# First projections read host-transposed rows, and the row norms are multiplied in afterwards

## The chip, the core and the metric

The kernel runs on one core of a Trainium2 chip, in one launch. The metric is device time in microseconds (us). An execution's time is a little longer than the span of its instructions: the profiled execution below took 1341.73 us and its span, from the first to the last instruction, is 1339.8 us. Engines go by the names of the profile: PE multiplies matrices, and PEld is its loading of weights; DVE is VectorE, ACT ScalarE, POOL GpSimd, and SP issues most transfers. PEclk is the clock that PE was granted, as a share of its higher level (1.00 is 2.4 GHz and 0.50 is 1.2 GHz).

## The reference

One layer of a streaming encoder over 1088 rows (1024 of a prompt, 64 of a sample) with 1024 features. Only its head matters here:

```python
def rmsnorm(x, g):
    y = x * lax.rsqrt(jnp.mean(x * x, axis=-1, keepdims=True) + EPS)
    return y * g
...
h = rmsnorm(x, g_mix)
c_q, c_kv, k_r, conv_b, conv_c, conv_x, gate_a, gate_c = split_cols(h @ w_in)
...
lat_new = rmsnorm(c_kv, g_ckv)
...
u = conv_c * conv_x
cv = sum(conv_w[k] * up[:, k:k + S] for k in range(CONV_W))   # up is u behind two earlier rows
y_c = (conv_b * cv) @ w_oc
...
m = jax.nn.sigmoid(gate_a) * y_a + jax.nn.sigmoid(gate_c) * y_c
```

Attention, an output projection, a mixture of 32 experts and a last gated embedding follow; the change leaves their code alone.

## The kernel before

**Tiles.** The 1088 rows are nine tiles of 128 rows (the last has 64). PE needs h with features on the partitions, so each tile is normalised and then transposed. The result lies in two pairs of buffers: hTA holds rows 0 to 383 (tiles 0, 1, 2; call it chunk A), hTB the rest (chunk B is rows 384 to 767, chunk C the last 320). Every fp32 operand is split into a rounded high part and a remainder (names with h and l at the end; `split`, `hi`, `lo`), and every product is three matmuls (`mm3`): high by high, low by high, high by low. `hi` is an ACT cast, `lo` a DVE subtraction.

**Steps of a tile i.** `A0` loads its rows (SP). `A1` squares and sums them on ACT (junk, L215), and POOL makes 1/rms in two instructions (rs, L85 and L86). `B` multiplies rows, 1/rms and the gain g_mix into hx (two DVE instructions; the gain is spread over the partitions beforehand by two matmuls of a row of ones with the gain, L256). `Tr` transposes hx by eight PE instructions (L237) into two banks of PSUM, and `C` splits them into hTA or hTB (two ACT casts, two DVE subtractions).

**Column tiles.** The projection's columns go through in groups of 128; `g_load` loads such a group g of w_in (w_r, 512 KB), `g_split` splits it, `g_mm` multiplies it with one chunk in 24 matmuls (eight blocks of features, three each). The first three groups are conv_c, conv_x and conv_b of the first 128 conv channels: I call their products c0, x0 and b0, with the chunk behind (c0A). They are copied, multiplied and convolved by `ev_c`, `ev_x` and `ev_b`; then a list of jobs does nine more conv groups and eight rounds of both gates (chunk A only, `ev_a` and `ev_g`). After that `L_mm` and `L_stat` make the latents, and their norms.

**What sets the order.** The text gives an order in which tiles, steps and matmuls mix by hand; a scheduler turns it into one queue for each engine, which the engine works off in order, and it decides which of the eight PSUM banks a product gets. A product whose bank is still to be read waits.

Of the kernel before, what the change touches and what calls it, by code (L numbers as in the profile page):

```python
# [7 lines left out]
F32 = mybir.dt.float32  # L8
# [3 lines left out]
AF = mybir.ActivationFunctionType  # L12
OP = mybir.AluOpType
# [7 lines left out]
D = 1024  # L21
KD = 8
# [12 lines left out]
A2 = 2 * T  # L35
DEEP = 5
WARM = 10


@with_exitstack  # L40
def body(ctx, tc, a):
# [35 lines left out]
    def split(p, raw, shape, tag, bufs, eng=None):  # L77
        h = p.tile(shape, F32R, name=tag + "h", tag=tag + "h", bufs=bufs)
        l = p.tile(shape, F32R, name=tag + "l", tag=tag + "l", bufs=bufs)
        hi(h, raw)  # L80
        lo(l, raw, h[:], eng)
        return h, l

    def rstd(out, ss, scale, n):
        nc.gpsimd.tensor_scalar(out=out, in0=ss, scalar1=scale, scalar2=EPS, op0=OP.mult, op1=OP.add)  # L85
        nc.gpsimd.tensor_tensor(out=out, in0=out, in1=mhalf[:out.shape[0], :n], op=OP.pow)  # L86

    def rstd_c(out, ss, cvec, n):
# [22 lines left out]
    def bank():  # L111
        return pb.tile([128, 512], F32, name="bk", tag="bk")
# [99 lines left out]
    def A1(i):
        junk = xp.tile([128, D], F32, name="junk")[:TN[i]]
        ss = xp.tile([128, 1], F32, name="ss", bufs=3)[:TN[i]]
        nc.scalar.activation(junk, xt_[i], AF.Square, accum_out=ss)  # L215
        rs_[i] = xp.tile([128, 1], F32, name="rs", bufs=3)[:TN[i]]
        rstd(rs_[i], ss, 1.0 / D, 1)

    hb_ = {}

    def B(i):
        hx = xp.tile([128, D], F32, name="hx", bufs=2)[:TN[i]]
        for b in range(2):
            c = slice(512 * b, 512 * b + 512)
            nc.vector.scalar_tensor_tensor(out=hx[:, c], in0=xt_[i][:, c], scalar=rs_[i], in1=gbk[b][:TN[i]],
                                           op0=OP.mult, op1=OP.mult)
        xt_.pop(i)
        hx_[i] = hx

    def Tr(i):  # L230
        hb_[i] = []
        for b in range(2):
            ps = bank()
            for j in range(4):
                k = 4 * b + j
                n = TN[i]
                nc.tensor.transpose(ps[:, 128 * j:128 * j + n], hx_[i][:, 128 * k:128 * k + 128], ident[:n, :n])  # L237
            hb_[i].append(ps)
        hx_.pop(i)

    def C(i):
        c0, n = 128 * i, TN[i]
        for b in range(2):
            v = hb_[i][b].rearrange("p (j n) -> p j n", j=4)[:, :, 0:n]
            xh, xl = hT(c0, n)
            hh = xh[:, 4 * b:4 * b + 4]
            hi(hh, v)
            lo(xl[:, 4 * b:4 * b + 4], v, hh)
            if n < 128:
                nc.gpsimd.tensor_copy(hB[0][:, 4 * b:4 * b + 4, T - TB:], xl[:, 4 * b:4 * b + 4].bitcast(F32))  # L250

    A0(0), A0(1), g_load(0), A0(2)
    A1(0), A1(1)
    gbk = [bank(), bank()]
    for b in range(2):
        nc.tensor.matmul(gbk[b], one1, grow[:, 512 * b:512 * b + 512], start=True, stop=True)  # L256
    B(0), A0(3), Tr(0), A1(2)
    B(1), Tr(1), C(0), g_load(1), A0(4), A1(3)
    g_split(0)
    B(2), Tr(2), C(1), A0(5), A1(4)  # L260
    B(3), C(2), A0(6)
    nc.sync.dma_start(stc, a["stateT"])
    nc.sync.dma_start(cw, a["convw"])
    fc, pc = ev_c(0), bank()
    g_mm(pc, *CH[0], wsp[0], hT, 0, 4, KD)
# [4 lines left out]
    fx, pxx = ev_x(0), bank()  # L270
    g_mm(pxx, *CH[0], wsp[1], hT, 0, 4, KD)
    Tr(5), B(6), C(5), A1(7)
    g_mm(pxx, *CH[0], wsp[1], hT, 4, 8, KD)
    Tr(6), B(7), C(6), A1(8)
    fx(pxx, *CH[0])
    pc = bank()
    g_mm(pc, *CH[1], wsp[0], hT, 0, 4, KD)
    Tr(7), B(8), C(7)
    g_mm(pc, *CH[1], wsp[0], hT, 4, 8, KD)
    Tr(8), C(8)  # L280
    fc(pc, *CH[1])
    xs_.close()
    pxx, pc = bank(), bank()
    g_load(2)
    g_mm(pxx, *CH[1], wsp[1], hT, 0, 8, KD)
    fx(pxx, *CH[1])
    g_split(2)
    pxx = bank()
# [157 lines left out]
    def L_stat(i):  # L446
        p1, p2 = st3[i]
        ss = lp.tile([128, 3], F32, name="ss3", bufs=2)
        cq = lp.tile([128, 256], F32, name="cq", bufs=2)
        ltk = lp.tile([128, 288], F32, name="ltk", bufs=2)  # L450
        if i == 8:
            fold(p1[:, 0:256], cq)
            fold(p2[:, 0:288], ltk)
        nc.scalar.activation(cq, p1[:, 0:256], AF.Square, accum_out=ss[:, 0:1])
        nc.scalar.activation(ltk[:, 0:256], p2[:, 0:256], AF.Square, accum_out=ss[:, 1:2])
        nc.scalar.activation(ltk[:, 256:288], p2[:, 256:288], AF.Square, accum_out=ss[:, 2:3])
        rs = lp.tile([128, 3], F32, name="rs3", bufs=2)
# [1352 lines left out]
```

## Time and profile before

| | |
|---|---|
| median of 3 runs | 1338.59 us (1335.41 to 1339.55) |
| profiled execution | 1341.73 us; span 1339.8 us |
| PE busy | 1272.8 us, 95% of the span |
| PEld, DVE, ACT, POOL busy | 82%, 63%, 49%, 24% |
| granted PE clock, mean | 0.986 |

The page of the profile cuts the span in 40 slices of 33.5 us. PE is busy for 7 tenths of the first one and of the 27th, for 8 of four others, and for 9 or more of all the rest. A row of a timeline gives an instruction's start and duration, the line of the program, the tile written and the tiles read, and in brackets how long its engine had been idle and what ended that.

### The profile page before, as it was taken

How to read it: one execution, taken by the hardware profiler on the slowest of the kernel's cores; microseconds unless marked ns; L12 is line 12 of the kernel's file. 1: busy time of each engine (PE TensorE's matmuls, PEld its weight loads, DVE VectorE, ACT ScalarE, POOL GpSimd, SP SyncE). 2: the span in 40 equal slices, each digit the busy share in tenths (PEclk: the TensorE clock that was granted, in tenths of full speed). 3: DMA queues.
4: the chain of work that ended last, by engine and by line, in shares of the span. 5: the costliest groups of instructions: out<-in, count | busy, mean ns of one | idle time of the engine just before them, and what ended most of it. 6: DMA issues, size and time to landing. Idle time of an engine off the chain costs nothing. (4 is left out here: it accounts for less than half of the span.)

```text
span 1339.8 us, 20433 instructions
## 1 busy us (share of the span) xinstructions
PE 1272.8 (95%) x7245; PEld 1102.1 (82%) x7245; DVE 842.7 (63%) x1629; ACT 650.1 (49%) x1278; POOL 317.9 (24%) x373
## 2 busy tenths in 40 slices
PE   7999999998998999999999999879999999999998
PEld 6999999998987988888999787656766666667886
DVE  6433243325684566666659756689898888874743
ACT  6221142213343455555545321258888888886322
POOL 2000011124663333343315200022222222210210
PEclk9999999999998999999999999989999999999999
DMA  5111298734477523242158656699999999957511
GB/s 199 64 46 34 79 361 299 277 111 142 133 191 231 166 80 126 68 154 90 54 191 275 237 220 213 237 309 353 352 352 347 335 357 347 351 183 280 196 40 55
DMA packets 106057, 272.36 MB, mean 203 GB/s; under 512 B 13521, under 2 KB 42689, under 8 KB 105922
## 3 DMA queue, kind: packets, MB, share of 16 engines
q1 hardware_dynamic: 89968, 220.29, 47.2%
q0 software_dynamic: 15840, 50.68, 11.8%
q8 instruction: 58, 0.95, 0.3%
q14 instruction: 45, 0.37, 0.1%
q10 hardware_dynamic: 146, 0.07, 0.0%
HBM read 211.14 MB, written 67.19 MB: 208 GB/s over the span
## 5 line engine op out<-in xcount | busy, mean ns | idle before, releaser
L60 DVE TENSOR_TENSOR wel<-eraw,weh 128x1024 fp32r<-128x1024 f32 x192 | 228.4, 1220 | 36.7 <-ACT weh L57 34.4
L57 ACT CAST weh<-eraw 128x1024 fp32r<-128x1024 f32 x192 | 195.2, 1054 | 12.9 <-PE bk L65 11.7
L770 POOL TENSOR_TENSOR P<-P,ri 128x128 f32<-128x128 f32 (+8 forms) x72 | 77.2, 1078 | 130.9 <-DVE ri L769 111.4
L63 PE MATMUL bk<-weh,xTh 128*96 128x512 f32 x256 | 103.2, 403 | 3.2 <-ACT xTh L57 1.9
L64 PE MATMUL bk<-wel,xTh 128*96 128x512 f32 x256 | 104.1, 407 | 1.3 <-DVE wel L60 1.2
L65 PE MATMUL bk<-weh,xTl 128*96 128x512 f32 x256 | 103.6, 405 | 0.0
L1360 POOL DMA_INDIRECT Yd<-y,idx x32 | 40.9, 1278 | 234.6 <-ACT y L1357 212.2
L60 DVE TENSOR_TENSOR wl<-w_r,wh 128x1024 fp32r<-128x1024 f32 x28 | 34.3, 1225 | 76.2 <-ACT wh L57 75.7
L63 PE MATMUL bk<-hTAh,wh 128*128 128x384 f32 x224 | 76.3, 340 | 1.4 <-ACT hTAh L57 1.4
L64 PE MATMUL bk<-hTAl,wh 128*128 128x384 f32 x224 | 76.2, 340 | 0.3 <-DVE hTAl L60 0.3
L65 PE MATMUL bk<-hTAh,wl 128*128 128x384 f32 x224 | 75.9, 339 | 0.0
L63 PE MATMUL fg<-hTBh,fw 128*128 128x384 f32 (+1 forms) x224 | 75.2, 336 | 0.3 <-ACT fgm L606 0.2
L57 ACT CAST wh<-w_r 128x1024 fp32r<-128x1024 f32 x28 | 29.4, 1050 | 92.4 <-PE bk L64 86.8
L65 PE MATMUL fg<-hTBh,fw 128*128 128x384 f32 (+1 forms) x224 | 73.6, 328 | 0.0
L64 PE MATMUL fg<-hTBl,fw 128*128 128x384 f32 (+1 forms) x224 | 73.3, 327 | 0.0
L63 PE MATMUL bk<-hTBh,wh 128*128 128x384 f32 (+1 forms) x192 | 62.2, 324 | 0.0
L64 PE MATMUL bk<-hTBl,wh 128*128 128x384 f32 (+1 forms) x192 | 62.0, 323 | 0.0
L65 PE MATMUL bk<-hTBh,wl 128*128 128x384 f32 (+1 forms) x192 | 61.8, 323 | 0.0
L64 PEld LDWEIGHTS bk<-wel,xTh 128*96 128x96 f32 x256 | 42.1, 164 | 21.7 <-DVE wel L60 7.1
L63 PEld LDWEIGHTS bk<-weh,xTh 128*96 128x96 f32 x256 | 41.8, 163 | 21.3 <-ACT xTh L57 3.4
L63 PE MATMUL bk<-weh,ath 128*96 128x512 f32 x128 | 51.0, 398 | 8.8 <-ACT ath L57 8.8
L756 DVE TENSOR_REDUCE nm<-S 128x1 f32<-128x128 f32 (+8 forms) x72 | 50.8, 706 | 13.0 <-PE S L65 11.9
(787 smaller groups left out, 3738.7 us busy)
## 6 DMA issues: line engine op xcount, KB each, us to landing
eraw<-in_we_dram SPq DMA_DIRECT2D x192, 512.0 KB
fw<-wsd POOLq DMA_DIRECT2D x32, 512.0 KB, 4.9
w_r<-in_wing_dram SPq DMA_DIRECT2D x28, 512.0 KB
gm_r<-gscr SPq DMA_DIRECT2D x16, 544.0 KB
wsd<-wh SPq DMA_DIRECT2D x16, 512.0 KB
wsd<-wl SPq DMA_DIRECT2D x16, 512.0 KB
xy<-Yd SPq DMA_DIRECT2D x16, 512.0 KB
vd<-V SPq DMA_DIRECT2D x10, 512.0 KB
```

The source lines that it names most:

```text
L57: nc.scalar.copy(dst, src)
L60: (eng or nc.vector).tensor_tensor(out=dst, in0=src, in1=h.bitcast(F32), op=OP.subtract)
L63: r = nc.tensor.matmul(ps, sh, mh, start=first, stop=False)
L64: nc.tensor.matmul(ps, sh, ml, start=False, stop=False)
L65: nc.tensor.matmul(ps, sl, mh, start=False, stop=last)
L756: nc.vector.tensor_reduce(out=nm, in_=s, axis=AX.XY, op=OP.max, negate=True)
L770: nc.gpsimd.tensor_tensor(out=P[:, :nk], in0=P[:, :nk], in1=ri.to_broadcast([128, nk]), op=OP.mult)
L1360: nc.gpsimd.indirect_dma_start(out=Yd[:, :], out_offset=bass.IndirectOffsetOnAxis(ap=col, axis=0), in_=buf, in_offset=None, bounds_check=A ...
```

## The change

Chunk A is no longer normalised before it is transposed. The host passes its 384 rows already transposed (xT) and the gain with features on the partitions (gmixT). `X0` loads two blocks of features of xT (384 KB), and `X1` multiplies by the gain and splits: ACT writes the high part, one DVE instruction the remainder. So hTA holds rows times gain without 1/rms, which is constant over a row of x and is now multiplied into the results: its square into c0 (`ev_c`; u is c times x), once into z in `ev_b`, once into each gate before the sigmoid, all by DVE with rb1 or rb2, which hold 1/rms and its square for each of the 384 rows on all partitions. `R(i)` makes them for tiles 0 to 2: squares on ACT, three POOL instructions, a diagonal matrix dg on DVE, and one matmul of ones with it. The latents' norms take the missing factor by a per-row EPS (epsv). Tiles 3 to 8 go through the old steps, with tile 5 transposed right behind tile 4. Ahead of all stand 14 matmuls of a 128x128 constant with itself. b0 is taken out of the list of jobs and done with c0 and x0; weight tiles have three buffers instead of two.

```diff
+WARM0 = 14
...
     def g_split(g):
-        wsp[g] = split(wp, wraw.pop(g), [128, KD, 128], "w", 2)
+        wsp[g] = split(wp, wraw.pop(g), [128, KD, 128], "w", 3)
...
         def f(ps, o, n):
-            nc.scalar.copy(csb[:, o:o + n], ps[:, :n])
+            if o < TB:
+                nc.vector.tensor_tensor(out=csb[:, o:o + n], in0=rb2, in1=ps[:, :n], op=OP.mult)
+            else:
+                nc.scalar.copy(csb[:, o:o + n], ps[:, :n])
...
+            if o < TB:
+                nc.vector.tensor_tensor(out=zf[:, o:o + n], in0=zf[:, o:o + n], in1=rb1, op=OP.mult)
...
+    def R(i):
+        junk = xp.tile([128, D], F32, name="junk")
+        ss = xp.tile([128, 1], F32, name="ss", bufs=3)
+        nc.scalar.activation(junk, xt_.pop(i), AF.Square, accum_out=ss)
+        rs = xp.tile([128, 1], F32, name="rs", bufs=3)
+        nc.gpsimd.tensor_scalar(out=ss, in0=ss, scalar1=1.0 / D, scalar2=EPS, op0=OP.mult, op1=OP.add)
+        nc.gpsimd.tensor_tensor(out=rs, in0=ss, in1=mhalf[:, :1], op=OP.pow)
+        nc.gpsimd.tensor_scalar(out=epsv[:, i:i + 1], in0=ss, scalar1=EPS, scalar2=0.0, op0=OP.mult, op1=OP.add)
+        dg = xp.tile([128, 128], F32, name="dg", bufs=2)
+        nc.vector.tensor_scalar(out=dg, in0=ident, scalar1=rs, scalar2=None, op0=OP.mult)
+        if i == 0:
+            rs_["b"] = bank()
+        nc.tensor.matmul(rs_["b"][:, 128 * i:128 * i + 128], one1, dg, start=True, stop=True)
+        if i == 2:
+            nc.scalar.copy(rb1, rs_["b"][:, 0:TB])
+            nc.scalar.activation(rb2, rs_["b"][:, 0:TB], AF.Square)
+
+    def X0(p):
+        xr_[p] = xp.tile([128, 2, TB], F32, name=f"xr{p}")
+        nc.sync.dma_start(xr_[p], a["xT"][:, 2 * p:2 * p + 2])
+
+    def X1(p):
+        r = xr_.pop(p)
+        for j in range(2):
+            k = 2 * p + j
+            nc.scalar.activation(hA[0][:, k], r[:, j], AF.Copy, scale=gmx[:, k:k + 1])
+            nc.vector.scalar_tensor_tensor(out=hA[1][:, k], in0=r[:, j], scalar=gmx[:, k:k + 1],
+                                           in1=hA[0][:, k].bitcast(F32), op0=OP.mult, op1=OP.subtract)
...
+    X0(0), g_load(0), X0(1), X0(2), X0(3), g_load(1)
+    A0(3), A0(4), g_load(2), A0(5), A0(0)
...
+    warm = bank()
+    for _ in range(WARM0):
+        nc.tensor.matmul(warm[:, 0:128], one1, one1, start=True, stop=True)
+    X1(0), g_split(0), X1(1)
...
+    g_mm(pc, *CH[0], wsp[0], hT, 0, 4, KD)
     gbk = [bank(), bank()]
...
+    X1(2), X1(3), g_split(1), A1(3)
     g_mm(pc, *CH[0], wsp[0], hT, 4, 8, KD)
-    Tr(4), B(5), C(4), A1(6), A0(8)
+    B(3), Tr(3), A1(4), A0(1)
+    g_mm(pxx, *CH[0], wsp[1], hT, 0, 8, KD)
+    g_split(2), C(3), B(4), Tr(4), A0(2), A1(5), C(4), B(5), Tr(5), R(0), C(5), A0(6)
+    pbb.append(bank())
+    g_mm(pbb[0], *CH[0], wsp[2], hT, 0, 8, KD)
+    R(1), R(2), A0(7)
     fc(pc, *CH[0])
...
         def f(ps, o, n):
-            nc.scalar.activation(gm[:, o:o + n], ps[:, :n], AF.Sigmoid)
+            nc.vector.tensor_tensor(out=gm[:, o:o + n], in0=rb1, in1=ps[:, :n], op=OP.mult)
+            nc.scalar.activation(gm[:, o:o + n], gm[:, o:o + n], AF.Sigmoid)
...
-    jobs = [("b", 0, 2)]
+    jobs = []
...
-        rstd_c(rs, ss, cnorm[:, 16:19], 3)
+        nc.gpsimd.tensor_tensor(out=rs, in0=ss, in1=cnorm[:, 16:19], op=OP.mult)
+        if i < 3:
+            nc.gpsimd.tensor_tensor(out=rs, in0=rs, in1=epsv[:, i:i + 1].to_broadcast([128, 3]), op=OP.add)
+        else:
+            nc.gpsimd.tensor_scalar(out=rs, in0=rs, scalar1=1.0, scalar2=EPS, op0=OP.mult, op1=OP.add)
+        nc.gpsimd.tensor_tensor(out=rs, in0=rs, in1=mhalf[:, :3], op=OP.pow)
```

Lines move by one in the helpers (L57 becomes L58, L63 to L65 become L64 to L66) and by more behind them. PE's queue began like this; bk is a PSUM bank, one is the tile of ones, grow the gain's row:

```order
L256 MATMUL bk<-grow,one_109 128x512 x2
L237 MATMUL bk<-ident,hx 128x128 x24
L63 MATMUL bk<-hTAh,wh 128x384
L64 MATMUL bk<-hTAl,wh 128x384
L65 MATMUL bk<-hTAh,wl 128x384
```

It now begins as follows; the rows left out are the rest of c0A's 24 matmuls, and the second pair of rows left out is x0A's 24:

```order
L300 MATMUL bk<-one_114 128x128 x14
L64 MATMUL bk<-hTAh,wh 128x384
L307 MATMUL bk<-grow,one_114 128x512 x2
L65 MATMUL bk<-hTAl,wh 128x384
L66 MATMUL bk<-hTAh,wl 128x384
...
L279 MATMUL bk<-ident,hx 128x128 x8
L64 MATMUL bk<-hTAh,wh 128x384
...
L279 MATMUL bk<-ident,hx 128x128 x16
L242 MATMUL bk<-dg,one_114 128x128
```

c0A stood behind the transposes of three tiles and stands now behind the constant matmuls; the gain's two matmuls stand inside c0A, and tile 3's eight transposes between c0A and x0A.

ACT's queue before, from its first square (junk) to the last cast into hTA:

```order
L215 ACTIVATE junk,ss<-xt 128x1024 x2
L57 CAST wh<-w_r 128x1024
L215 ACTIVATE junk,ss<-xt 128x1024
L57 CAST wh<-w_r 128x1024
L57 CAST hTAh<-bk 128x4x128 x4
L215 ACTIVATE junk,ss<-xt 128x1024
L57 CAST hTAh<-bk 128x4x128 x2
```

ACT's queue now. L226 squares a tile from 3 on, L233 one of tiles 0 to 2 (in `R`); L244 and L245 write rb1 and rb2:

```order
L58 CAST wh<-w_r 128x1024
L257 ACTIVATE hTAh<-xr_116,gmx 128x384 x2
...
L58 CAST wh<-w_r 128x1024
L226 ACTIVATE junk,ss<-xt 128x1024 x3
L58 CAST hTBh<-bk 128x4x128 x2
L233 ACTIVATE junk,ss<-xt 128x1024
...
L226 ACTIVATE junk,ss<-xt 64x1024
L244 COPY rb_89<-bk 128x384
L245 ACTIVATE rb_90<-bk 128x384
L170 COPY csb<-bk 128x384
```

The first square of a tile stands now behind two weight casts and all eight casts of hTA, and rb2, without which c0A's bank can't be emptied, stands behind the squares of all nine tiles.

## Rows read from the trace of the kernel before

**Rows 1.** Windows of 40 us: start:end, length, busy us of each engine, PEclk.

```profile
0.00:40.00 40.00, 31.97 (x167) 27.61 (x168) 25.86 (x42) 24.00 (x42) 7.69 (x25) 0.96 0.49 173
40.00:80.00 40.00, 40.00 (x248) 40.00 (x247) 13.35 (x22) 8.49 (x13) 0.00 (x0) 1.00 0.18 60
```

**Rows 2.** PE's timeline at the start: start, duration, instruction, idle time before.

```profile
5.04 3.75 PE L256 MATMUL bk<-grow,one 1*128 1x512 f32 x4 [5.04 <-DMA grow<-in_gbig_dram]
...
16.75 0.44 PE L63 MATMUL bk<-hTAh,wh 128*128 128x384 f32 x1 [1.45 <-ACT hTAh L57]
17.47 0.45 PE L64 MATMUL bk<-hTAl,wh 128*128 128x384 f32 x1 [0.28 <-DVE hTAl L60]
```

**Rows 3.** PE's timeline in the first stage, at both clock levels.

```profile
18.84 0.52 PE L63 MATMUL bk<-hTAh,wh 128*128 128x384 f32 x1
19.16 0.52 PE L64 MATMUL bk<-hTAl,wh 128*128 128x384 f32 x1
...
22.46 0.34 PE L63 MATMUL bk<-hTAh,wh 128*128 128x384 f32 x1
...
23.85 0.34 PE L65 MATMUL bk<-hTAh,wl 128*128 128x384 f32 x1
...
29.97 1.04 PE L237 MATMUL bk<-ident,hx 128*128 128x128 f32 x8
...
58.34 0.31 PE L65 MATMUL bk<-hTBh,wl 128*128 128x320 f32 x1
...
59.80 0.34 PE L63 MATMUL bk<-hTAh,wh 128*128 128x384 f32 x1
```

**Rows 4.** Timeline of ACT and POOL at the start.

```profile
4.72 1.06 ACT L215 ACTIVATE junk<-xt 128x1024 f32<-128x1024 f32 x1 [1.72 <-DMA xt<-in_x_dram]
...
6.10 1.06 ACT L215 ACTIVATE junk<-xt 128x1024 f32<-128x1024 f32 x1 [0.23 <-DMA xt<-in_x_dram]
...
7.69 1.05 ACT L57 CAST wh<-w_r 128x1024 fp32r<-128x1024 f32 x1 [0.44 <-DMA w_r<-in_wing_dram]
...
9.01 1.06 ACT L215 ACTIVATE junk<-xt 128x1024 f32<-128x1024 f32 x1 [0.28 <-DMA xt<-in_x_dram]
...
10.25 0.19 POOL L85 TENSOR_SCALAR rs<-ss 128x1 f32<-128x1 f32 x1 [2.09 <-ACT junk L215]
...
10.52 0.55 POOL L86 TENSOR_TENSOR rs<-rs,mhalf 128x1 f32<-128x1 f32 x1
```

**Rows 5.** Groups of ACT and DVE in the first 59.7 us: count, busy us, mean ns.

```profile
L57 ACT CAST hTBh<-bk 128x512 fp32r<-128x512 f32 x10 | 5.4, 586 | 3.3 <-PE bk L237 3.3
L57 ACT CAST zTh<-zf 128x384 fp32r<-128x384 f32 x2 | 1.0, 514 | 6.7 <-DVE zf L194 6.7
L225 DVE SCALAR_TENSOR_TENSOR hx<-xt,rs,bk 128x512 f32<-128x512 f32 x16 | 11.3, 741 | 7.1 <-PE bk L256 6.2 <-issue 0.5 <-POOL rs L86 0.3
L60 DVE TENSOR_TENSOR wl<-w_r,wh 128x1024 fp32r<-128x1024 f32 x4 | 4.9, 1221 | 4.0 <-ACT wh L57 3.9
L60 DVE TENSOR_TENSOR zTl<-zf,zTh 128x384 fp32r<-128x384 f32 x2 | 1.1, 559 | 1.1 <-ACT zTh L57 1.1
```

**Rows 6.** POOL beside DVE, where the latents' norms are made.

```profile
288.76 0.96 DVE L60 TENSOR_TENSOR wuq0l<-wup_r,wuq0h 128x768 fp32r<-128x768 f32 x1 [1.00 <-ACT wuq0h L57]
...
289.36 0.41 POOL L89 TENSOR_TENSOR rs<-ss,cnorm 128x3 f32<-128x3 f32 x1 [7.40 <-ACT ltk L456]
...
302.32 0.19 POOL L89 TENSOR_TENSOR rs<-ss,cnorm 128x3 f32<-128x3 f32 x1 [1.31 <-ACT ltk L456]
```

**Rows 7.** Windows with PEclk as the last but two: 1 us at the start, 10 us late.

```profile
17.00:18.00 1.00, 0.72 (x4) 0.53 (x4) 1.00 (x3) 1.00 (x2) 0.13 (x1) 0.99 0.96 385
18.00:19.00 1.00, 1.00 (x5) 1.00 (x4) 1.00 (x3) 0.26 (x2) 0.57 (x2) 0.50 0.43 172
...
21.00:22.00 1.00, 1.00 (x9) 0.92 (x8) 0.00 (x0) 0.13 (x1) 0.74 (x2) 0.80 0.73 254
...
1212.00:1222.00 10.00, 7.86 (x28) 6.01 (x28) 2.08 (x2) 2.96 (x6) 0.00 (x0) 0.83 0.67 217
```

More of the change, by code (lines that the diff above doesn't have):

```diff
@@ L117, in body @@
     hA = [hp.tile([128, KD, TB], F32R, name=f"hTA{n}") for n in "hl"]
+    rb1 = hp.tile([128, TB], F32, name="rb1")
+    rb2 = hp.tile([128, TB], F32, name="rb2")
+    epsv = hp.tile([128, 3], F32, name="epsv")
     def hT(o, n):
@@ L128, in body @@
     zTl = zp.tile([128, 4, T], F32R, name="zTl")
-    ws, wp = opened("win", bufs=2, side="right")
+    ws, wp = opened("win", bufs=3, side="right")
     wraw = {}
@@ L201, in body @@
     nc.scalar.dma_start(ident, a["ident"])
+    gmx = xp.tile([128, KD], F32, name="gmx")
+    nc.scalar.dma_start(gmx, a["gmixT"])
     grow = xp.tile([1, D], F32, name="grow")
     nc.scalar.dma_start(grow, a["gbig"][0:1, :])
-    one1 = xp.tile([1, 128], F32, name="one1")
+    one1 = xp.tile([128, 128], F32, name="one1")
     nc.vector.memset(one1, 1.0)
@@ L208, in A0 @@
     def A0(i):
-        xt_[i] = xp.tile([128, D], F32, name="xt", bufs=3)[:TN[i]]
+        xt_[i] = xp.tile([128, D], F32, name="xt", bufs=4)[:TN[i]]
         nc.sync.dma_start(xt_[i], a["x"][128 * i:128 * i + TN[i]])
@@ L217, in A1 @@
         rstd(rs_[i], ss, 1.0 / D, 1)
+    def R(i):
[14 more added lines that the diff above has]
+            nc.scalar.activation(rb2, rs_["b"][:, 0:TB], AF.Square)
+    xr_ = {}
+    def X0(p):
[8 more added lines that the diff above has]
+                                           in1=hA[0][:, k].bitcast(F32), op0=OP.mult, op1=OP.subtract)
     hb_ = {}
@@ L250, in C @@
                 nc.gpsimd.tensor_copy(hB[0][:, 4 * b:4 * b + 4, T - TB:], xl[:, 4 * b:4 * b + 4].bitcast(F32))
-    A0(0), A0(1), g_load(0), A0(2)
-    A1(0), A1(1)
+    X0(0), g_load(0), X0(1), X0(2), X0(3), g_load(1)
+    A0(3), A0(4), g_load(2), A0(5), A0(0)
+    nc.sync.dma_start(stc, a["stateT"])
+    nc.sync.dma_start(cw, a["convw"])
+    warm = bank()
+    for _ in range(WARM0):
+        nc.tensor.matmul(warm[:, 0:128], one1, one1, start=True, stop=True)
+    X1(0), g_split(0), X1(1)
+    fc, fx = ev_c(0), ev_x(0)
@@ L254, in body @@
+    pc, pxx, pbb = bank(), bank(), []
+    g_mm(pc, *CH[0], wsp[0], hT, 0, 4, KD)
     gbk = [bank(), bank()]
     for b in range(2):
[L256 to L265, printed above, removed]
@@ L266, in body @@
-    Tr(3), g_split(1), A1(5), B(4), C(3), A0(7)
-    g_mm(pc, *CH[0], wsp[0], hT, 4, 8, KD)
-    Tr(4), B(5), C(4), A1(6), A0(8)
-    fc(pc, *CH[0])
[L270 to L274, printed above, removed]
-    fx(pxx, *CH[0])
[L276 to L280, printed above, removed]
-    fc(pc, *CH[1])
@@ L282, in body @@
-    xs_.close()
[L283 to L288, printed above, removed]
+        nc.tensor.matmul(gbk[b], one1[0:1], grow[:, 512 * b:512 * b + 512], start=True, stop=True)
+    X1(2), X1(3), g_split(1), A1(3)
+    g_mm(pc, *CH[0], wsp[0], hT, 4, 8, KD)
+    B(3), Tr(3), A1(4), A0(1)
+    g_mm(pxx, *CH[0], wsp[1], hT, 0, 8, KD)
+    g_split(2), C(3), B(4), Tr(4), A0(2), A1(5), C(4), B(5), Tr(5), R(0), C(5), A0(6)
@@ new lines, in body @@
+    pbb.append(bank())
+    g_mm(pbb[0], *CH[0], wsp[2], hT, 0, 8, KD)
+    R(1), R(2), A0(7)
+    fc(pc, *CH[0])
+    fx(pxx, *CH[0])
+    A0(8)
+    pc, pxx = bank(), bank()
+    g_mm(pc, *CH[1], wsp[0], hT, 0, 8, KD)
+    A1(6)
+    B(6), Tr(6), C(6)
+    fc(pc, *CH[1])
+    g_mm(pxx, *CH[1], wsp[1], hT, 0, 8, KD)
+    A1(7)
+    B(7), Tr(7), C(7)
+    fx(pxx, *CH[1])
+    A1(8)
+    pbb.append(bank())
+    g_mm(pbb[1], *CH[1], wsp[2], hT, 0, 8, KD)
+    B(8), Tr(8), C(8)
+    xs_.close()
+    pc, pxx = bank(), bank()
@@ L289, in body @@
+    g_load(3)
     g_mm(pc, *CH[2], wsp[0], hT, 0, 8, KD)
     fc(pc, *CH[2])
-    g_load(3)
     g_mm(pxx, *CH[2], wsp[1], hT, 0, 8, KD)
     fx(pxx, *CH[2])
+    g_split(3)
+    g_load(4)
+    pbb.append(bank())
+    g_mm(pbb[2], *CH[2], wsp[2], hT, 0, 8, KD)
+    fb = ev_b(0)
+    for p, c in zip(pbb, CH):
+        fb(p, *c)
     gs_ = {}
@@ L316, in f @@
         def f(ps, o, n):
-            nc.scalar.activation(gm[:, o:o + n], ps[:, :n], AF.Sigmoid)
+            nc.vector.tensor_tensor(out=gm[:, o:o + n], in0=rb1, in1=ps[:, :n], op=OP.mult)
+            nc.scalar.activation(gm[:, o:o + n], gm[:, o:o + n], AF.Sigmoid)
         return f
@@ L1708, in pack @@
     A["x"] = np.concatenate([f("x_prompt")[0], f("x_sample")[0]], 0)
+    A["xT"] = np.ascontiguousarray(A["x"][:TB].reshape(TB, 8, 128).transpose(2, 1, 0))
+    A["gmixT"] = np.ascontiguousarray(f("g_mix")[0].reshape(8, 128).T)
     w = f("w_in")[0]
```

## The prediction

> **What bounds the kernel now.** I first read the windows [rows 1]. Before 40 us PE is busy for 31.97 of 40 us; from 40 to 80 us it has no gap, while DVE works for 13.35 us of 40 and ACT for 8.49. PE is the bound, so what counts at the start is how late it gets into its dense stream and at what clock. The end of b0 is a point that both kernels share, as the work behind it is the same. Before, the next product starts at 59.80 us [rows 3].
>
> How much of that was needed? At the full clock a 384-column matmul starts every 0.174 us (eight steps from 22.46 to 23.85) and a 320-column one every 0.146 us (ten from 58.34 to 59.80) [rows 3]. c0, x0 and b0 are 72 matmuls on each chunk: 72 x (0.174 + 0.174 + 0.146) = 35.6 us. The other 24.2 us are waits, transposes of nine tiles and slow clock.
>
> The timeline of the start shows the waits: PE has nothing to do until 5.04 us, then spreads the gain for 3.75 us, transposes, and begins c0A at 16.75 us after a gap of 1.45 us and another of 0.28 us [rows 2]. Then the clock falls: the one-us windows grant 0.99 at 17 us, 0.50 from 18 us, 0.80 at 21 us [rows 7], so some 3.4 us at the lower of its two levels (1.2 instead of 2.4 GHz). The reader sees it in the steps too: 0.32 us from 18.84 to 19.16 [rows 3]. It cost half of 3.4, 1.7 us.
>
> **The change, part by part.** I follow the new order of the queues up to x0A, from where on PE should have no gap.
>
> *Loads.* In the old order 512 KB, 1024, 1536 and 2048 KB have come when ACT goes on at 4.72, 6.10, 7.69 and 9.01 us, each time after a wait for that load [rows 4]: 1.43 us for each 512 KB. The first xT pair and weight tile are 896 KB: 4.72 + 0.75 x 1.43 = 5.8 us. The second weight tile (2560 KB) is there at 10.4 us, tile 3 (3072 KB) at 11.9.
>
> *ACT.* A weight cast takes 1.05 us [rows 4]: 5.8 to 6.85. Eight casts of 384 columns with the gain are not in the trace. The nearest is a plain one of the same size, 0.514 us [rows 5]; a 512-column cast from PSUM with 0.586 bounds them from above: 4.1 to 4.7 us, I take 4.1, so 10.95. Second weight cast to 12.0, square of tile 3 (1.06) to 13.1. None of these waits for its load.
>
> *DVE.* Remainder of the first weight tile 1.221 us [rows 5], 6.9 to 8.1; eight remainders of hTA at 0.559 (the same size without the gain; the form with a scalar takes 0.741 on 512 columns from PSUM), so 4.5 to 5.9 us, I take 4.5: 12.6. Second weight remainder to 13.8.
>
> *PE.* The constant matmuls are new: 128 columns of fp32. A gain matmul of 512 columns takes 3.75 / 2 = 1.88 us at the start [rows 2], a quarter is 0.47, so 14 take 6.6 us from about 1.1 us if the clock stays low, and 3.3 if it were full. Either way they end (4.4 to 7.7) about when c0A's first operands come (7.4), so they cost nothing. The gain's two matmuls stand behind c0A's first one: 1.9 us at the full clock, hidden, as c0A then follows DVE's remainders, 0.559 us each against three matmuls of 0.52. c0A ends at 13.0. Before, c0A began at 16.75.
>
> *The wait that takes its place.* Tile 3's transposes stand ahead of x0A in PE's queue, and need 1/rms and hx. POOL starts 0.18 us behind the square (9.01 + 1.06 to 10.25) with 0.19 and 0.55 us [rows 4]. DVE is at the second weight remainder then. Beside such a subtraction of two SBUF tiles POOL's short instruction took 0.41 us instead of 0.19 [rows 6]. So 13.1 + 0.18 + 0.41 + 0.08 + 0.55 = 14.3, hx's first half at 15.1, the second at 15.85. PE has nothing between 13.0 and 15.1 us; x0A, whose weights are ready at 13.8, stands behind. Tile 3 is through at 16.4, and x0A starts.
>
> The Trainium skill (SBUF — State Buffer, Who interferes with whom) says that a VectorE instruction with two SBUF inputs blocks a GpSimd instruction that reads SBUF until it ends. By it POOL would wait until 13.8 and x0A would start some 0.1 us later. The trace agrees: the 0.41 us end at 289.77, DVE's subtraction at 289.72.
>
> *From x0A to the end of b0.* Five products of 24 x 0.174 (20.9), three of 24 x 0.146 (10.5), five transposed tiles at 1.04 [rows 3] (5.2; the last is smaller, which I leave for hand-overs), three dg matmuls at half of 0.47 (0.7): 37.3 us. 16.4 + 37.3 = 53.7 against 59.80: **6.1 us** less.
>
> *The clock.* The gap of 2.1 us and a second of 0.2 are like those that stood before the falls in this trace: 1.45 and 0.28 us ahead of 18 us, and late in the kernel 2.14 us of 10 idle with a mean of 0.83 granted [rows 7], which is again 3.4 us at 0.50. I take one fall, at about 15 to 17 us, inside the dense stream: **1.7 us** back. None is the lower bound, two the upper (3.4).
>
> *Costs at nothing.* DVE's 20 more multiplications with rb1 (4 in z, 16 gates) and 4 with rb2, at 0.56 us each, lie under products of 4.2 us: DVE has 26 of 40 us free there [rows 1]. If PE had to wait for each it would be 13 us. The 1.5 MB of xT push tiles 3 to 8 back by 4.3 us on the queue, but ACT, not the load, paces them, as above. b0 before the job list only changes places. POOL's sum with epsv has the form that takes 0.19 to 0.41 us [rows 6] for one of 0.19 [rows 4], thrice. The scheduler also mixed the last experts' matmuls anew: nothing speaks for either sign; the nearest gap there is 2.14 us [rows 7], so plus or minus 2.
>
> **Sum.** 6.1 - 1.7 = 4.4 us off the profiled execution's 1341.73, 1337.3. That execution lies 3.1 us above the median of the runs, which I take to hold after the change too: 1338.59 - 4.4 = **1334.2**.
>
> **The rivals.**
> *The clock stays up in the gap.* Then all 6.1 us come: 1332.5. For it: a free-running judgement may split the gap; the rows show only falls, after as little idle time as 1.73 us. Chance 0.2.
> *The clock is low in c0A*, because the constant matmuls end too early and PE waits for its first operands. Then the gain takes 3.75 us from 7.4 on, c0A 24 x 0.32 = 7.7 us [rows 3], to 18.9, and x0A starts at 19.95, 3.55 late, but at the full clock: 6.1 - 3.55 = 2.55 off, 1336.0. Chance 0.1.
> *The gain is lost later*, in the experts' stage, if it kept to its loads' times: 1338.6. Against it: those loads are issued from a queue in order, behind earlier work, and should move forward with it. Chance 0.1.
> *Slower: the late squares hold PSUM.* x0B needs the bank of c0A, whose emptying needs rb2, behind all squares on ACT. ACT: tile 3's casts (2 x 0.586) to 17.1, tile 0's square to 18.4, weights 19.4, tile 4's casts behind its transposes 22.3, then tile 1, tile 5's casts, and tiles 2, 6, 7, 8 at 1.25 us, to 29.7, rb1 and rb2 30.7, DVE 31.3. PE asks for the bank at 16.4 + 4.2 + 2.3 + 4.2 + 4.7 + 1.0 = 32.8. Slack 1.5 us. Every us beyond it costs one; slower by 4 us needs 1.5 + 4.4 + 4.0 = 9.9 us more, say by loads of tiles 6 to 8 that wait for their buffers: 1342.6 or more. Chance 0.07.
> The main case has 0.45; the last 0.08 is a re-mixed end that gives some us.
>
> **How the numbers follow.** About 0.3% (4.0 us) is what a measurement of this kernel can tell from no change, so 1334.6 is the line, and the forecast lies just beyond it. Faster: 0.27 of the main case, 0.2 with the clock up, 0.05 of the last: 0.52. Same: 0.18 + 0.1 + 0.1 + 0.03 = 0.41. Slower 0.07. The range goes from 1330.5 (clock up, and 2 us from the end) to 1339.0 (all lost); the main case alone holds 1332.5 to 1336 (no fall to two).
>
> **What would show it.** In the changed profile: constant matmuls from about 1 us; c0A between 7.4 and 13; a PE gap of about 2 us ended by DVE's hx; x0A at 16.4; half clock for 3.4 us behind it; the first product behind b0 at about 55.4; hardly a PE wait between. I am wrong if c0A steps at 0.32 us, if PE waits at x0B for csb, or if that point comes early and the end doesn't.

## The result, and the profile after

The changed kernel took 1331.86 us (median of 11 runs, 1327.64 to 1333.49) against 1340.28 us (11 runs, 1335.41 to 1343.47): a ratio of 0.9936, 95% interval 0.9923 to 0.9948, so 8.4 us less (6.9 to 10.3). The forecast was 4.4 us less, 1334.2. The side and the stated range hold; the size is about half. The profiled execution has a span of 1329.5 us, 10.3 less than the one of before.

The windows of 40 us, columns as in [rows 1], show PE filled from the start:

```profile
0.00:40.00 40.00, 38.42 (x210) 36.24 (x211) 24.77 (x42) 24.77 (x43) 7.88 (x26) 0.96 0.63 226
40.00:80.00 40.00, 39.79 (x252) 39.39 (x251) 16.49 (x32) 11.21 (x16) 1.25 (x2) 1.00 0.18 60
```

PE's timeline of the changed kernel answers to [rows 2, 3]: the constant matmuls, c0A's first, the gain, two of c0A's slow steps, tile 3's transposes, x0A's first, x0B's first, and the last of b0 with the first product behind it:

```profile
1.04 6.16 PE L300 MATMUL bk<-one 128*128 128x128 f32 x28 [1.04 <-DVE u L176]
7.54 0.44 PE L64 MATMUL bk<-hTAh,wh 128*128 128x384 f32 x1 [0.34 <-ACT hTAh L257]
7.91 1.98 PE L307 MATMUL bk<-grow,one 1*128 1x512 f32 x4
...
10.56 0.53 PE L65 MATMUL bk<-hTAl,wh 128*128 128x384 f32 x1
10.88 0.53 PE L66 MATMUL bk<-hTAh,wl 128*128 128x384 f32 x1
...
15.49 1.03 PE L279 MATMUL bk<-ident,hx 128*128 128x128 f32 x8
16.29 0.42 PE L64 MATMUL bk<-hTAh,wh 128*128 128x384 f32 x1
...
32.87 0.42 PE L64 MATMUL bk<-hTBh,wh 128*128 128x384 f32 x1
...
53.74 0.30 PE L66 MATMUL bk<-hTBh,wl 128*128 128x320 f32 x1
53.88 0.34 PE L64 MATMUL bk<-hTAh,wh 128*128 128x384 f32 x1
```

x0A starts at 16.29 us (forecast 16.4), and the first product behind b0 at 53.88, 5.92 us ahead of before. Between c0A and tile 3's transposes there is no idle time: the gain ahead of its second matmul and its steps of 0.32 us say why c0A lasts until 15.49. The one-us windows show its clock (PEclk is the last but two, as in [rows 7]); by the shares of the two outer windows it falls to the lower of its two levels (1.2 instead of 2.4 GHz) at 10.30 us and is back at 13.70:

```profile
10.00:11.00 1.00, 1.00 (x5) 1.00 (x6) 1.00 (x3) 1.00 (x4) 0.00 (x0) 0.65 1.01 410
11.00:12.00 1.00, 1.00 (x5) 1.00 (x4) 1.00 (x3) 1.00 (x3) 0.00 (x0) 0.50 1.05 426
12.00:13.00 1.00, 1.00 (x5) 1.00 (x4) 1.00 (x2) 1.00 (x2) 0.00 (x0) 0.50 1.00 401
13.00:14.00 1.00, 1.00 (x6) 1.00 (x5) 0.60 (x1) 0.97 (x2) 0.81 (x2) 0.65 1.05 422
```

The chain to tile 3's rows, on ACT, POOL and DVE, with the emptying of c0A's bank (csb) last:

```profile
5.93 1.04 ACT L58 CAST wh<-w_r 128x1024 fp32r<-128x1024 f32 x1 [2.44 <-DMA w_r<-in_wing_dram]
6.88 4.15 ACT L257 ACTIVATE hTAh<-xr,gmx 128x384 fp32r<-128x384 f32 x8
11.87 1.05 ACT L226 ACTIVATE junk<-xt 128x1024 f32<-128x1024 f32 x1
13.11 0.54 POOL L86 TENSOR_SCALAR rs<-ss 128x1 f32<-128x1 f32 x1 [12.28 <-ACT junk L226]
8.15 4.31 DVE L258 SCALAR_TENSOR_TENSOR hTAl<-xr,gmx,hTAh 128x384 fp32r<-128x384 f32 x8
14.33 2.72 DVE L267 SCALAR_TENSOR_TENSOR hx<-xt,rs,bk 128x512 f32<-128x512 f32 x4 [0.73 <-POOL rs L87]
31.08 0.55 DVE L168 TENSOR_TENSOR csb<-rb,bk 128x384 f32<-128x384 f32 x1 [0.87 <-ACT rb L245]
```

So 5.9 of the profiled 10.3 us are there at the end of the first stage. Matmul by matmul beside the trace of before, the lead slips to 5.64 us by 301.79 us (307.43 before), and is 11.30 at 303.56 us (314.86 before). What happened there is on three engines. Kernel before, SP's issue of the last up-projection weight, ACT's cast of it, POOL's issue of four loads for the later gates' weights (fw, 4 x 512 KB), and the row of PE's waits:

```profile
302.34 0.33 SPq L630 DMA_DIRECT2D wup_r<-in_wukv_dram  x1
308.89 1.04 ACT L57 CAST wukv1h<-wup_r 128x1024 fp32r<-128x1024 f32 x1 [5.83 <-DMA wup_r<-in_wukv_dram]
298.77 2.24 POOL L587 DMA_DIRECT2D fw<-wsd  x4 [2.85 <-PE bk L65]
PE bk L63 <- ACT qn L521: 4.0, 1, 4.0
```

The changed kernel, the same three instructions (PE has no such wait):

```profile
295.62 0.33 SPq L689 DMA_DIRECT2D wup_r<-in_wukv_dram  x1
298.78 1.05 ACT L58 CAST wukv1h<-wup_r 128x1024 fp32r<-128x1024 f32 x1 [2.45 <-DMA wup_r<-in_wukv_dram]
296.94 2.21 POOL L646 DMA_DIRECT2D fw<-wsd  x4
```

Before, the 2 MB were issued 3.6 us ahead of the weight, and it took 6.5 us from issue to cast; after, they were issued 1.3 us behind it, and it took 3.2. PE's 4.0 us of waiting went, and with them the fall of the clock that followed in the kernel before:

```profile
311.00:312.00 1.00, 0.27 (x1) 0.30 (x2) 1.00 (x4) 0.61 (x4) 0.63 (x3) 0.76 0.00 0
312.00:313.00 1.00, 1.00 (x3) 0.81 (x3) 0.89 (x5) 0.05 (x1) 0.60 (x1) 0.50 0.00 0
313.00:314.00 1.00, 1.00 (x3) 0.72 (x3) 0.64 (x2) 0.72 (x2) 0.00 (x0) 0.50 0.43 146
314.00:315.00 1.00, 1.00 (x4) 0.80 (x3) 1.00 (x3) 0.33 (x1) 0.00 (x0) 0.53 0.03 9
```

What is missing to 1.00 in the column of PEclk adds up to 1.7 us. With the wait that is 5.7, which is what the lead grew by. In POOL's queue the loads had changed places with the norm of the latents' third tile.

### The profile page after: what moved, and what is told of

Its sections match the earlier page's. It is cut to its first block, busy times and chain, and to the rows that moved or that the text cites. A ratio compares the mean times of both kernels' runs of the same rounds, so it can differ in the third digit from the quotient of the medians.

```text
span 1329.5 us, 20478 instructions
## 1 busy us (share of the span) xinstructions
PE 1268.9 (95%) x7255; PEld 1100.2 (83%) x7255; DVE 854.9 (64%) x1652; ACT 650.6 (49%) x1278; POOL 319.4 (24%) x376
## 5 line engine op out<-in xcount | busy, mean ns | idle before, releaser
L58 ACT CAST weh<-eraw 128x1024 fp32r<-128x1024 f32 x192 | 195.5, 1054 | 10.9 <-PE bk L66 10.9
L65 PE MATMUL bk<-wel,xTh 128*96 128x512 f32 x256 | 103.6, 405 | 2.0 <-DVE wel L61 1.7
L64 PE MATMUL bk<-weh,xTh 128*96 128x512 f32 x256 | 102.3, 400 | 2.4 <-ACT xTh L58 1.7
L66 PE MATMUL bk<-weh,xTl 128*96 128x512 f32 x256 | 102.6, 401 | 0.0
L64 PE MATMUL bk<-hTAh,wh 128*128 128x384 f32 x224 | 76.3, 341 | 0.5 <-ACT hTAh L257 0.3
L65 PE MATMUL bk<-hTAl,wh 128*128 128x384 f32 x224 | 76.1, 340 | 0.0
L66 PE MATMUL bk<-hTAh,wl 128*128 128x384 f32 x224 | 75.9, 339 | 0.0
L64 PE MATMUL fg<-hTBh,fw 128*128 128x384 f32 (+1 forms) x224 | 74.5, 333 | 0.3 <-ACT fgm L665 0.2
L66 PE MATMUL fg<-hTBh,fw 128*128 128x384 f32 (+1 forms) x224 | 72.9, 326 | 0.0
L65 PE MATMUL fg<-hTBl,fw 128*128 128x384 f32 (+1 forms) x224 | 72.7, 325 | 0.0
L58 ACT CAST wh<-w_r 128x1024 fp32r<-128x1024 f32 x28 | 29.4, 1051 | 87.5 <-issue 42.4
L64 PE MATMUL bk<-hTBh,wh 128*128 128x384 f32 (+1 forms) x192 | 62.0, 324 | 0.2 <-ACT hTBh L58 0.2
L65 PE MATMUL bk<-hTBl,wh 128*128 128x384 f32 (+1 forms) x192 | 62.0, 323 | 0.0
L66 PE MATMUL bk<-hTBh,wl 128*128 128x384 f32 (+1 forms) x192 | 61.9, 323 | 0.0
L65 PEld LDWEIGHTS bk<-wel,xTh 128*96 128x96 f32 x256 | 41.6, 163 | 22.2 <-DVE wel L61 7.9
L64 PE MATMUL bk<-weh,ath 128*96 128x512 f32 x128 | 51.0, 398 | 8.9 <-ACT ath L58 8.8
L64 PEld LDWEIGHTS bk<-weh,xTh 128*96 128x96 f32 x256 | 41.5, 162 | 20.6 <-ACT xTh L58 3.1
```

The costliest lines, as they stand in the source:

```text
L64: r = nc.tensor.matmul(ps, sh, mh, start=first, stop=False)
L65: nc.tensor.matmul(ps, sh, ml, start=False, stop=False)
L66: nc.tensor.matmul(ps, sl, mh, start=False, stop=last)
```

## The experiments

"Behind b0" is the start of the first product behind b0 in a run's trace; before 59.80, changed 53.88. Each result gives the median, its ratio to the kernel before on the same chip and, in brackets, the 95% interval.

**1. No constant matmuls.** `WARM0 = 0` in the changed kernel.

> The changed kernel without its 14 matmuls on a constant; the count of steps is the same otherwise. Theory A (they only raise the clock): the gain's two matmuls, which now meet a PE that has done nothing, take about 3.75 us as before the change instead of 1.9, and the first product c0A runs at least in part in steps of 0.32 us. c0A then ends at 16.7 to 18.7 us instead of 15.5, and the first product behind b0 starts 1.2 to 3.2 us later than 53.88 us; time 1333 to 1335. Rival B (the constant matmuls are idle work, since tile 3's normalised rows set when x0A starts): that product starts within 0.3 us of 53.88 and the time stays at 1331.9.

1335.68 us, ratio to before 0.9967 (0.9949 to 0.9985); behind b0 56.45, 2.6 us later. The gain took 3.78 us, c0A went in half-rate steps until 17 us, and tile 3's transposes began at 18.31. Theory A, a little over its time. Rows of this run, two of c0A's matmuls and the window that holds them:

```profile
13.51 0.52 PE L64 MATMUL bk<-hTAh,wh 128*128 128x384 f32 x1
13.83 0.52 PE L65 MATMUL bk<-hTAl,wh 128*128 128x384 f32 x1
...
13.00:14.00 1.00, 1.00 (x5) 1.00 (x4) 0.47 (x1) 1.00 (x2) 0.92 (x2) 1.00 1.03 414
```

The steps are 0.32 us, yet the column says 1.00: at the start of the program the granted clock in the windows doesn't tell the rate, the steps do. So the constant matmuls are worth 2.6 us at that place, by the rate at which the gain and c0A run.

**2. Only the constant matmuls, in the kernel before.** `one1` gets 128 partitions, and 14 matmuls stand ahead of the gain's.

> The kernel before with the 14 constant matmuls ahead of the gain's and nothing else of the change. Theory A (the gain in the first stage comes from the transposed rows, which let c0A start at 7.5 us): c0A still waits for the norm, DVE and the transposes and starts within 0.7 us of 16.75, the first product behind b0 within 1 us of 59.80, or 1.7 earlier if the clock no longer falls at 18 us; time 1338 to 1340. Rival B (the constant matmuls are what pays, by the clock): 3 us or more earlier at that place, time below 1337.5.

1341.20 us, 1.0009 (0.9999 to 1.0019); c0A at 17.55, behind b0 60.68. Rival B falls. The gain's matmuls were faster (1.98 us), but stood behind the constant ones and ended at 8.7, as before. Theory A's own bounds are narrowly missed (c0A 0.80 us behind 16.75 for 0.7, and 1341.20 for 1340). The early start of c0A needs the transposed rows.

**3. Only POOL's order, in the kernel before.**

```
-  nc.gpsimd.dma_start(fw[j][s]..., wsd[j, s])
+  r = nc.gpsimd.dma_start(fw[j][s]..., wsd[j, s])
+  if j == 0:
+      tc.add_manual_dep(r.ins, last3[2].ins.name, ...)   # last3[i]: the power that ends tile i's norm
```

> The kernel before with one wait added: the first four loads that POOL issues for the later gates' weights (2 MB) stand behind the norm of the latents' third tile in POOL's queue, where they stand in the changed kernel, and not ahead of it. Theory A (some 4 to 5 us of the change's gain come from this order: the 2 MB no longer go ahead of the last up-projection weight, which PE waits for at 307 us): ACT's wait for that load falls from 5.8 us to about 2.5, PE's wait of 4.0 us at 307 us goes or falls below 1 us, PE is 3 to 5.5 us earlier at 315 us, and the time is 1335 to 1337.5. Rival B (that wait went because PE came earlier, or by chance): PE still waits 3 us or more there, time 1339 to 1341.

1334.26 us, 0.9960 (0.9946 to 0.9975): 6.0 us from one wait, with the first stage as before (behind b0 59.95). ACT's wait for the weight was 3.10 us, PE's 4.0 us wait was gone, and PE was 5.5 us earlier at the place of 314.86. Theory A, with a time a little below its range.

**4. The gain by a load.** `gb`, 512 KB behind tile 3's rows, replaces the gain's two matmuls in the changed kernel.

> The changed kernel with the gain spread over the partitions by a load of 512 KB behind tile 3's rows instead of by two matmuls, which takes 1.9 us of work off PE ahead of c0A's second matmul. Theory A (from c0A's end on PE waits for tile 3's normalised rows, which come at 15.0 us by ACT's square, POOL and DVE): x0A starts only 0.3 to 0.6 us earlier than 16.29, a gap of about 1 to 1.5 us appears ahead of tile 3's transposes, and the first product behind b0 is at most 0.6 us earlier than 53.88. Rival B (PE's own work and its clock set that place): c0A ends at 13.6, x0A starts at 14.4, and the first product behind b0 starts at 52.0.

1334.79 us, 0.9964 (0.9944 to 0.9984). x0A at 16.06, 0.23 earlier, behind a gap of 0.49 us that hx ended; behind b0 52.91, 0.97 earlier. c0A's clock fell here too (from 8.7 to 12.1 us), which filled a part of the gap that theory A expected. x0A lies near theory A, the stage's end between the two, and the time is no shorter: inconclusive.

**5. epsv elsewhere.** One word in the changed kernel:

```
-  epsv = hp.tile([128, 3], F32, name="epsv")
+  epsv = keep.tile([128, 3], F32, name="epsv")
```

> The changed kernel with its three columns of epsv in the pool that lives through the whole program, not in that of hTA's rows. PE's, ACT's and SP's orders stay as they are; in POOL's queue the four loads of the later gates' weights (2 MB), which land in hTA's place, no longer have to wait until the norm of the latents' third tile has read epsv, and stand ahead of it again, as before the change. Theory A (some 5 us of the change's gain are a by-product of where epsv was put): PE waits about 4 us for the query's squares near 300 us, which the changed kernel doesn't, the first product on the key and value weights starts 4 to 6 us later than its 303.56 us, and the time is 1335.5 to 1338. Rival B (the start alone pays, and what came behind it is chance): no such wait, 1331 to 1333.

1337.29 us, 0.9976 (0.9963 to 0.9989). No instruction of PE or ACT and no load of SP changed its place, but POOL's queue did (changed kernel -, this +):

```
 TENSOR_TENSOR rs<-rs,mhalf 128x3
+DMA fw<-wsd 128x1024
+DMA fw<-wsd 128x1024
+DMA fw<-wsd 128x1024
+DMA fw<-wsd 128x1024
 TENSOR_TENSOR rs<-ss,cnorm 128x3
 TENSOR_TENSOR rs<-rs,epsv 128x3
 TENSOR_TENSOR rs<-rs,mhalf 128x3
-DMA fw<-wsd 128x1024
-DMA fw<-wsd 128x1024
-DMA fw<-wsd 128x1024
-DMA fw<-wsd 128x1024
```

The reason is in lines that the diff doesn't touch: `hs.close()` gives back the memory of hTA's pool, and `fgp` with fw is opened in it. The change had put epsv into that pool, and the third tile's norm reads it, so the 2 MB had to wait for that norm. With epsv elsewhere they go first again, and the waits are back. PE's row, and ACT's, of this run:

```profile
PE bk L64 <- ACT qn L580: 2.3, 1, 2.3
ACT wukv1h L58 <- DMA wup_r<-in_wukv_dram: 6.3, 1, 6.3
```

Theory A: the median is in its range, while the wait (2.3 for 4) and the delay (3.7 us for 4 to 6) are a little short in this execution.

**6. Two buffers for the raw weights, in the kernel before.** `bufs=1` becomes `bufs=2` for `wup_r`, so that the last load needn't wait until the one ahead is split.

> The kernel before with two buffers instead of one for the raw up-projection weights, so that their last load doesn't wait for the one ahead to be split; POOL's order is that of before. Theory A (PE's 4 us at 307 us came from this load standing behind the 2 MB): the load is in before the 2 MB start, PE's wait goes, PE is 4 to 5.5 us earlier at 315 us, time 1335 to 1336.5. Rival B (it is not the load but the 2 MB themselves, or POOL's place in the chain of the norms): PE still waits 2 us or more, time 1338 to 1341.

1332.72 us, 0.9950 (0.9931 to 0.9969). Both key-and-value weights were issued at 289.50, ahead of the 2 MB; PE's wait was gone. Theory A for the wait; the time is below its range. It is 8.0 us below the kernel before, so this one edit gains about as much as the whole change. The profiled execution also had no fall of the clock in the first stage (behind b0 58.72); whether that holds for the other three executions isn't shown.

**7. The gain by a load, and x0A ahead of tile 3's transposes.** Run 4's edit in the changed kernel, and the line `B(3), Tr(3), A1(4), A0(1)` behind x0A's `g_mm`.

> The changed kernel with the gain spread by a load of 512 KB, as in the run above, and tile 3's transposes behind x0A instead of ahead of it. Theory A (what sets x0A is tile 3's normalised rows, and PE has no other work until then): with x0A ahead, it starts at 13.7 to 14.6 us, behind c0A and the second weight's remainder, PE has no gap over 0.3 us before 40 us, and the first product behind b0 starts 1.2 to 2.0 us earlier than 53.88; time 1329 to 1331. Rival B (c0A's pace or its clock, or the transposed rows later on, set the end of the stage): less than 0.6 us earlier there, 1331.5 to 1333.

1333.39 us, 0.9946 (0.9933 to 0.9959); x0A at 12.06 us, 4.2 earlier, behind b0 53.69, 0.19 earlier. Theory A falls. The stage's end is where rival B has it, but not by c0A's clock, which stayed at 1.00 in this execution. PE lost its lead before the third weight's product; PE's rows with their waits, and DVE's row for that weight's remainder:

```profile
21.29 0.46 PE L241 MATMUL bk<-dg,one 128*128 128x128 f32 x2 [0.77 <-DVE dg L238]
21.93 0.44 PE L64 MATMUL bk<-hTAh,wh 128*128 128x384 f32 x1 [0.18 <-ACT wh L58]
23.53 0.44 PE L66 MATMUL bk<-hTAh,wl 128*128 128x384 f32 x1 [0.67 <-DVE wl L61]
22.26 1.22 DVE L61 TENSOR_TENSOR wl<-w_r,wh 128x1024 fp32r<-128x1024 f32 x1
```

In the changed kernel this remainder begins at 19.75. What sets the stage's end in this run is thus the preparation on ACT and DVE up to the third weight, not when x0A starts.

**8 to 11. The two causes crossed, on one chip.** The kernel of run 5 again; that kernel with two buffers; the changed kernel with two buffers; and the changed kernel itself. PE's order is the same in all four.

> The kernel with epsv in the lasting pool once more, for a second profile and for times on one chip beside the three runs that follow. Its first profiled execution took 1331.42 us where its median was 1337.29. Theory A (the 2 MB ahead of the last up-projection load cost PE a wait whose length changes with the load's luck): the second profile shows the wait near 302 us again, 2 to 5 us long, and the median is again 1335.5 to 1338. Rival B (that median was this chip's luck): 1331 to 1333.5.

> The kernel with epsv in the lasting pool and two buffers for the raw up-projection weights; PE's order is that of the changed kernel. Theory A (POOL's order matters only because the last up-projection load stands behind the 2 MB): with that load issued ahead of them, PE has no wait for the query's squares near 302 us and the first key and value product starts within 1 us of 302.19 us, although POOL's order is the old one; time 1331 to 1333.5, as the changed kernel. Rival B (the 2 MB cost something else when they come early, as through the traffic behind them): 1335 to 1338, as with one buffer.

> The changed kernel with two buffers for the raw up-projection weights. Theory A (in the changed kernel PE no longer waits for that load at all): nothing to gain, within 0.15% of the changed kernel run beside it. Rival B (ACT's wait of 2.5 us for the load still delays PE through the chain of the later tiles): 2 us or more faster than it, below 1330.

> The changed kernel itself on the chip of the three runs above, as their base. It should come out at 1331 to 1333, some 4 to 6 us below the one with epsv in the lasting pool.

| | one buffer | two buffers |
|---|---|---|
| epsv in the lasting pool (2 MB first) | 1336.56, 0.9965 (0.9951 to 0.9979) | 1329.91, 0.9926 (0.9901 to 0.9951) |
| epsv with hTA (2 MB behind the norm) | 1333.65, 0.9940 (0.9920 to 0.9960) | 1332.15, 0.9935 (0.9914 to 0.9956) |

Run 8 again shows PE's wait (2.8 us) and ACT's (6.52). Run 11 lies 2.9 us below run 8, not the 4 to 6 expected, and their intervals overlap. Run 5, on another chip, lay 5.4 us above the changed kernel, and there the intervals are apart (from 0.9963, up to 0.9948). With two buffers POOL's order no longer hurts: in run 9 PE has no wait there, as theory A said, and its time is lower than theory A's. SP's issue of both loads, POOL's of the 2 MB, and PE's first product on the new weights in run 9:

```profile
285.01 1.60 SPq L689 DMA_DIRECT2D wup_r<-in_wukv_dram  x2
292.79 2.21 POOL L646 DMA_DIRECT2D fw<-wsd  x4 [0.98 <-PE bk L66]
301.67 0.39 PE L64 MATMUL bk<-wukv0h,latTh 128*128 128x512 f32 x1
```

Run 10 gains nothing that can be told from run 11 (0.11%). Run 9 has the lowest median of all, but its interval overlaps that of the changed kernel.

Run 11 and the first profile of the changed kernel are the same program, with spans of 1335.6 and 1329.5 us. Windows of 10 us, the first kernel's execution and then run 11's:

```profile
367.00:377.00 10.00, 9.81 (x55) 9.29 (x56) 9.44 (x28) 6.04 (x15) 5.33 (x5) 1.00 0.50 149
500.00:510.00 10.00, 9.58 (x67) 8.74 (x66) 6.25 (x16) 5.99 (x16) 4.68 (x6) 1.00 0.56 190
```

```profile
367.00:377.00 10.00, 9.37 (x46) 9.19 (x46) 9.33 (x28) 5.07 (x13) 5.32 (x5) 0.83 0.48 141
500.00:510.00 10.00, 8.81 (x49) 7.96 (x50) 5.60 (x14) 5.19 (x14) 4.08 (x4) 0.83 0.41 130
```

The clock falls in both stretches of the second and in neither of the first. Up to PE's last work, 1 minus the granted clock, summed over one-us windows, is 15.3 us in the first and 22.2 in the second: 6.9 us, for 6.1 us of span. So two profiles of single executions can't be set against each other to better than some 6 us as a whole; the places where they part can be.

## Why the prediction was right in side and wrong in size

In brackets stands what was forecast.

- **Loads, ACT, DVE and POOL.** The first cast began at 5.93 (5.8), eight casts took 4.15 us (4.1), the remainders 4.31 (4.5), tile 3's square began at 11.87 (12.0), hx was written from 14.33 (14.3). POOL's first instruction took 0.54 us (0.41) beside DVE's second weight remainder. Prices taken from plain casts of the same size held.
- **Constant matmuls.** They ended at 7.20 (4.4 to 7.7). "They cost nothing" held; that they bring 2.6 us was only in the rival "the clock is low in c0A", which run 1 brought about.
- **c0A until 13.0.** It lasted until 15.49. The gain's 1.98 us weren't hidden: they delayed c0A's second matmul to 9.82 (8.65 in run 4, where they are gone), and the clock's fall at 10.30 took another 1.7 us.
- **The gap of 2.1 us ahead of tile 3, and a clock fall in the dense stream behind it.** Neither came: the fall came in c0A, in time that PE would else have spent waiting for hx, which was there at 15.0, so it cost only some 0.5 us. x0A started at 16.29 (16.4), in part by luck, as slow work stood where the wait was forecast. From there to behind b0 it took 37.6 us (37.3), and the 1.7 us weren't given back: 5.9 instead of 4.4. In run 8 the fall in c0A lasted from 9.3 to 16.2 us, and behind b0 was 55.35, the forecast's 55.4 by another way: how long the fall lasts changes from execution to execution.
- **"Costs at nothing": POOL's sum with epsv.** This is the step that failed. I priced its duration (0.20 us, as forecast) and not where its operand lies. Sharing hTA's memory held four loads back by one norm, and that took away a wait of 4 us and a clock fall. The times: without it (runs 5 and 8) the change gains 3.5 and 4.6 us, with it 8.4 and 7.6. That 3.5 and 4.6 lie about the 4.4 forecast is in part luck: 5.9 us were there at the stage's end, and some were lost behind it.
- **The sum.** About 4 us from the first stage and 3 to 5 from the place of epsv (2.9 between runs 8 and 11, 5.4 between run 5 and the changed kernel). In the kernel before, POOL's order alone gave 6.0 (run 3) and two buffers alone 8.0 (run 6), so the gains don't add up. Behind either of these edits the rest of the change brings only some 2 to 3 us: 0.9936 against run 3's 0.9960, and 0.9926 (run 9) or 0.9935 (run 10) against run 6's 0.9950, each with overlapping intervals. So some of the first stage's lead is lost further on. A part of that shows in the profile, where PE waits 6.28 us at 402 us for keys that come back from memory, while the kernel before waited 4.81 at the same place for DVE (the changed kernel first, then the one before):

```profile
402.65 1.03 PE L764 MATMUL tp<-ident,ks__4073 128*64 128x128 f32 x4 [6.28 <-DMA ks__4073<-knd]
411.90 0.42 PE L705 MATMUL tp<-ident,ks__4045 128*64 128x128 f32 x1 [4.81 <-DVE kT L60]
```

In the six profiled executions with the changed kernel's order of PE this wait is between 4.06 and 6.28 us long. Whether that is all isn't settled, nor why the times of run 5's kernel spread from 1331.42 to 1340.92 us.

- **The rivals.** "The clock stays up" is what the sum came to, not by its mechanism. "The gain is lost later" held for some of the 5.9, but not where it was placed: 0.3 us of the lead had gone by 302 us and 1.5 went at 402, while from 900 to 1300 us the lead kept between 9.5 and 10.0 us. "The late squares hold PSUM" didn't come: csb was done at 31.63 for x0B's 32.87, a slack of 1.24 us (1.5). That each us beyond it costs one wasn't tried.

## What to carry to other kernels

A new small tile takes part in the lifetime of its pool: before adding one, look at what is opened in that memory next, and at which loads then wait for its last reader. Where a load waits for a buffer and a bigger load can get ahead of it, a second buffer (4 KB a partition here) removed the dependence on the order (runs 9 and 10); alone in the kernel before, it gained as much as the whole change (run 6). Starting x0A 4.2 us earlier was worth 0.2 us at the stage's end, as the engines that prepare the third weight were still at it (run 7).

## What the runs showed of the hardware

- The granted clock fell with PE busy: at 10.30 us in the changed kernel's first profile, after 0.34 us of idle time since 1.04 us, and at 10.6 us in run 5 after none. Ahead of both falls PE had done the constant matmuls, one matmul of c0A, the gain's matmuls of one row (1.98 us) and the next few matmuls of c0A. All six profiled executions with this order of PE show a fall between 9.3 and 10.6 us. The falls of the kernel before all had 0.85 us or more of idle time in the five us ahead of them. The Trainium skill (TensorE: Matmul & The Clock Gate, What's actually happening) has the clock go back to the lower level after idleness; the rows at 10 us don't show that idleness, and the measurement decides. What brings this fall stays open: without the gain's matmuls it came in run 4, at 8.7 us behind idle times of 0.95 and 0.84 us, and not in run 7, behind 0.57 and 0.83. Run 5, whose first row has PE busy for all of 5 us:

```profile
5.00:10.00 5.00, 5.00 (x19) 3.37 (x18) 3.25 (x5) 4.33 (x8) 0.00 (x0) 1.00 1.03 413
10.00:11.00 1.00, 1.00 (x7) 1.00 (x6) 1.00 (x3) 1.00 (x3) 0.00 (x0) 0.79 1.02 406
```

- Nor does the length of the idle time alone decide. In run 11 the clock fell at 368 and 501 us, behind 1.89 and 0.85 us of idle time; the first execution of the same program idled for 1.75 and 0.85 us at these places and kept 1.00. The first execution's rows, then run 11's:

```profile
367.19 0.41 PE L64 MATMUL bk<-hTBh,fw 128*128 128x384 f32 x1 [1.75 <-issue]
498.87 0.64 PE L776 MATMUL tp<-ident,qs__4609 128*96 128x128 f32 x4 [0.85 <-DVE PlA L61]
```

```profile
367.63 0.41 PE L64 MATMUL bk<-hTBh,fw 128*128 128x384 f32 x1 [1.89 <-issue]
500.51 0.64 PE L776 MATMUL tp<-ident,qs__4609 128*96 128x128 f32 x4 [0.85 <-DVE PlA L61]
```

- At the start of the program, half-rate steps (0.32 us) stand beside a granted clock of 1.00 (run 1). That PE starts at the lower level until it has worked, as the same section of the Trainium skill says, the steps agree with.
